# The products of the modulation vectors on VectorE, one multiply-add per piece, instead of two GpSimd operations

## The chip, the cores and the metric

The kernel runs on one core of a Trainium2 chip. The metric is the device time of one execution in microseconds. Three runs of the kernel before took 4000.06, 3992.86 and 4002.28 us; their median is 4000.06 us.

## What is computed

Two model blocks follow each other on one sequence of 512 tokens and 1024 channels, all in float32. The first has a feed-forward part, a mixer (chunked attention beside a gated recurrence) and a second feed-forward part. The second has two layers, each a mixer of four branches (Fourier, differential attention, grouped attention, convolution) and a feed-forward part; beside it runs a context sequence of 256 tokens. Each of the parts is wrapped in a normalisation whose shift, scale and gate are vectors that depend on a conditioning vector alone:

```
c_act = silu(c)
mod = (c_act @ w_ada[l] + b_ada[l]).reshape(b, N_SUB, 3, D_MODEL)
...
def sandwich(x, fn, g_pre, g_post, shift, scale, gate, res_w):
    h = modulate(rmsnorm(x, g_pre), shift, scale)
    y = rmsnorm(fn(h), g_post)
    return x + res_w * gate[:, None, :] * y
...
mod_x = (jax.nn.silu(c) @ w_mod[l] + b_mod[l])[:, None, :]
mod_c = (jax.nn.silu(c_ctx) @ w_mod[l] + b_mod[l])[None, None, :]
```

A modulation vector is thus one row of 1024 numbers: a vector of 1024 times a matrix of 1024x1024. The kernel computes 29 of them. The first two are made in a start routine (L392) that the change leaves alone; the other 27 go through `mod` and `pieces`.

## The kernel before

**Matrix products.** Each float32 weight is split in two: a high part (`whi`, written by ScalarE, L282) and the rest (`wlo`, written by VectorE as raw minus high, L283), and each product is three matmuls (L309 to L311, or L321 to L323). The work is a list of `Step`s; a step owns units of weights of 128x1024. `run` (L226) goes through the steps and calls `pump` (L235), which loads units ahead into five `raw` tiles (`RAWB`, L161; the DMA is issued on SyncE's queue, L243) and splits them up to four ahead (`HB`, L162). A `raw` tile is free again when its last reader is done; for a split unit that is the VectorE subtraction of L283.

**A modulation vector.** The matrix is cut in eight pieces of 128 rows, each loaded as one unit of 128x1024 that is not split (`plain`, L390), into the same five `raw` tiles. Piece i is multiplied by column i of the activated conditioning vector (`csil`, one number per partition) and added to an accumulator `a`, a tile `s` of 128x1024. When the eighth piece is in, `turn` (L348) transposes the accumulator in blocks of 32x32 and adds along the row on VectorE (L352, L353), and `fin` (L355) ends it with one matmul, the bias and the gain (L360, L363) and writes the vector to memory by a DMA of GpSimd's queue (L365). `use` (L469) later loads it back, broadcast over the partitions.

**How a piece is multiplied.** `pieces` (L371) takes the engine as an argument and has a branch for either:

```
if i == 0:
    eng.tensor_scalar(a, v, c, 0.0, ALU.mult, ALU.add)
elif eng is self.DVE:
    eng.scalar_tensor_tensor(a, v, c, a, ALU.mult, ALU.add)
else:
    eng.tensor_scalar(v, v, c, 0.0, ALU.mult, ALU.add)
    eng.tensor_tensor(a, a, v, ALU.add)
```

Before the change `mod` passes GpSimd (`self.POOL`, L366): the first piece is one operation (L383), the other seven are two each (L387 into the `raw` tile, L388 into the accumulator). The `raw` tile is free after L388.

**What sets the order.** The vectors of one part are woven between the steps of the part before it (`weave`, L138, by the costs and the shares in `TUNE`). A scheduler then orders the instructions of each engine when the program is built, so a change of one operation's engine can move others. Beside the pieces GpSimd does a taps part of the convolution (L1539, L1540), small powers for the normalisations (L335, L481), some scalings (L1343, L867) and its DMAs, all in one queue.

**Other lines that the prediction names.** L1149 and L1147 are parts of the rotary embedding on VectorE; L328 is the rest of a split of a matmul's result (`esplit`, reads PSUM); L334, L335 and L1440 are a normalisation's factor (VectorE, then GpSimd, then VectorE) that the matmul of L1445 needs; L906 and L908 are the first part's short convolution; L930 to L945 its recurrence.

Of the kernel before, what the change touches and what calls it, by code (L numbers as in the profile page):

```python
# [159 lines left out]
class K:  # L160
# [177 lines left out]
    def mod(self, key, w, c0, bias, ccol, gain=None, mult=None):  # L338

        E, DVE, PE = self.E, self.DVE, self.PE  # L340

        def begin():
            self.cnt += 1
            r = E[key, "r"] = self.sb.tile([32, 2, 32], F32, tag="row", bufs=3, name=f"row{self.cnt}")
            for j, v in enumerate([bias[c0:c0 + D]] + ([gain] if gain is not None else [])):
                self.POOL.dma_start(out=r[:, j, :], in_=v.rearrange("(a b) -> a b", a=32))

        def turn(raw):  # L348

            a, v = E.pop((key, "a")), raw[:, 0, :]  # L350
            q = E[key, "q"] = self.sb.tile([128, 32], F32, tag="red", bufs=3, name=f"red{self.cnt}")
            DVE.transpose(v, a)  # L352
            DVE.tensor_reduce(q, v.rearrange("p (a b) -> p a b", b=32), AX, ALU.add)  # L353

        def fin():  # L355
            q, r = E.pop((key, "q")), E.pop((key, "r"))
            ps = self.mm((32,))[0:32, :]
            PE.matmul(ps, q, self.fold, start=True, stop=True)
            v = r[:, 0, :]
            DVE.tensor_tensor(v, ps, v, ALU.add)  # L360
            if gain is not None:
                o = (1.0, ALU.add) if mult is None else (mult, ALU.mult)
                DVE.scalar_tensor_tensor(v, v, o[0], r[:, 1, :], o[1], ALU.mult)  # L363
            d = E[key, "d"] = self.dr.tile([32, 32], F32, tag="d" + key, name="d" + key)
            self.POOL.dma_start(out=d, in_=v)  # L365
        steps = self.pieces(key, w, c0, ccol, begin, self.POOL)  # L366
        u = steps[-1].units
        steps[-1].units, steps[-1].borrow = [], u
        return steps + [Step(turn, u, need=(), pe=0.1), Step(fin, pe=0.1)]
# [113 lines left out]
    def border(self, xk, T, yk=None, out=None, norm=None, hk=None):  # L483
# [34 lines left out]
        def tr(t):  # L518
# [14 lines left out]
            for g in range(2):  # L533
                if T == S:
                    self.esplit(ps[g], hT[:, 0, 4 * g:4 * g + 4, ts], hT[:, 1, 4 * g:4 * g + 4, ts])
                else:
                    for q in range(2):
                        self.esplit(ps[g][:, 2 * q:2 * q + 2, :], hT[2 * g + q][:, 0, :, ts], hT[2 * g + q][:, 1, :, ts])
        return first, mod, tr

    def calls(self, *cs, **kw):
# [1414 lines left out]
```

## Time and profile before

| | |
|---|---|
| median of three runs | 4000.06 us (3992.86 to 4002.28) |
| the profiled execution's own time | 4003.47 us |
| its span, first to last instruction | 4001.7 us |
| mean granted TensorE clock | 0.964 of 2.4 GHz |
| TensorE matmuls (PE) busy | 3773.1 us, 94% |
| VectorE (DVE) busy | 2514.3 us, 63% |
| ScalarE (ACT) busy | 1533.9 us, 38% |
| GpSimd (POOL) busy | 1394.0 us, 35% |
| memory traffic | 133 GB/s over the span |

The engines run beside each other; an engine's busy time counts its instructions alone, and its idle time is waiting. A chain of waits says which engine the end hangs on; here it is TensorE nearly throughout. The granted clock is the share of full speed that TensorE was allowed in a stretch; it has two levels, full (2.4 GHz) and half (1.2 GHz), so a mean of 0.9 means that a fifth of the stretch was at half.

### The profile page before, as it was taken

What the parts mean: (1) busy time and instruction counts of PE and PEld (TensorE: products, weight loads), DVE (VectorE), ACT (ScalarE), POOL (GpSimd) and SP (SyncE); (2) the same over time, 40 slices, a digit from 0 to 9 for tenths busy, and PEclk for the clock granted to TensorE, in tenths of its full rate; (3) what the DMA queues carried; (4) which work ended last, traced back from release to release, by engine and by line L of the source; (5) the groups of instructions that cost most, each with busy time, mean ns of one, the idle gap of its engine ahead of it and who ended that gap; (6) DMA issues with size and microseconds to landing.
All of it is one profiled execution on the core that took longest, in us unless ns stands there. A gap on an engine that the chain in (4) does not pass through costs nothing. (4 is left out here: it accounts for less than half of the span.)

```text
span 4001.7 us, 50668 instructions
## 1 busy us (share of the span) xinstructions
PE 3773.1 (94%) x19612; PEld 3196.3 (80%) x19612; DVE 2514.3 (63%) x3347; ACT 1533.9 (38%) x2437; POOL 1394.0 (35%) x1133
## 2 busy tenths in 40 slices
PE   7999987999899999899999989999998999899999
PEld 5888866778788887778887878888887887688887
DVE  5343478846766665957667466767587776655344
ACT  4222345533354443235433334333332543334322
POOL 1341364315844332451323144543146132312100
PEclk9999988999999999999999989999999999899999
DMA  6554533446455655221333356666532123333432
GB/s 226 155 160 128 152 113 116 145 127 194 149 160 173 187 168 176 80 82 41 106 95 95 121 166 198 195 200 195 170 104 82 56 85 96 106 121 114 127 103 94
DMA packets 534050, 536.26 MB, mean 134 GB/s; under 512 B 19696, under 2 KB 435696, under 8 KB 533808
## 3 DMA queue, kind: packets, MB, share of 16 engines
q1 hardware_dynamic: 517088, 487.48, 40.1%
q0 software_dynamic: 16720, 45.53, 3.5%
q8 instruction: 154, 2.52, 0.3%
q14 instruction: 88, 0.72, 0.1%
HBM read 507.66 MB, written 25.28 MB: 133 GB/s over the span
## 5 line engine op out<-in xcount | busy, mean ns | idle before, releaser
L283 DVE TENSOR_TENSOR wlo<-raw,whi 128x1024 fp32r<-128x1024 f32 (+3 forms) x674 | 921.9, 1370 | 803.1 <-ACT whi L282 783.6
L282 ACT ACTIVATE whi<-raw 128x1024 fp32r<-128x1024 f32 (+3 forms) x674 | 694.1, 1032 | 1551.6 <-PE mm L310 649.5
L309 PE MATMUL mm<-hT,whi 128*128 128x512 f32 (+1 forms) x2384 | 910.8, 385 | 44.4 <-ACT hT L326 11.0
L310 PE MATMUL mm<-hT,whi 128*128 128x512 f32 (+1 forms) x2384 | 907.1, 382 | 17.9 <-DVE hT L328 17.9
L311 PE MATMUL mm<-hT,wlo 128*128 128x512 f32 (+1 forms) x2384 | 902.9, 380 | 0.0
L309 PEld LDWEIGHTS mm<-hT,whi 128*128 128x128 f32 x2384 | 460.4, 195 | 132.4 <-ACT hT L326 14.0
L310 PEld LDWEIGHTS mm<-hT,whi 128*128 128x128 f32 x2384 | 463.2, 195 | 99.3 <-DVE hT L328 20.5
L311 PEld LDWEIGHTS mm<-hT,wlo 128*128 128x128 f32 x2384 | 462.6, 194 | 83.4 <-issue 0.4
L388 POOL TENSOR_TENSOR s<-s,raw 128x1024 f32<-128x1024 f32 x189 | 495.6, 2622 | 15.8
L387 POOL TENSOR_SCALAR raw<-raw,csil 128x1024 f32<-128x1024 f32 x189 | 281.4, 1489 | 380.9 <-DMA raw<-in_w_mod 191.2
L322 PE MATMUL mm<-wlo,s 128*128 128x512 f32 (+1 forms) x1004 | 371.4, 371 | 4.6 <-DVE wlo L283 4.6
L321 PE MATMUL mm<-whi,s 128*128 128x512 f32 (+1 forms) x1004 | 369.1, 371 | 0.0
L323 PE MATMUL mm<-whi,s 128*128 128x512 f32 (+1 forms) x1004 | 368.9, 370 | 0.0
L309 PE MATMUL mm<-s,whi 128*128 128x256 f32 (+1 forms) x1032 | 338.1, 329 | 10.9 <-ACT s L910 5.1
L310 PE MATMUL mm<-s,whi 128*128 128x256 f32 (+1 forms) x1032 | 333.1, 323 | 3.0 <-DVE s L328 3.0
L311 PE MATMUL mm<-s,wlo 128*128 128x256 f32 (+1 forms) x1032 | 332.0, 322 | 0.0
L309 PEld LDWEIGHTS mm<-s,whi 128*128 128x128 f32 x1032 | 199.2, 193 | 31.7 <-ACT s L910 5.5
L326 ACT ACTIVATE s<-mm 128x512 fp32r<-128x512 f32 (+2 forms) x302 | 156.7, 548 | 172.6 <-PE mm L1027 67.8
L322 PEld LDWEIGHTS mm<-wlo,s 128*128 128x128 f32 x1004 | 189.8, 189 | 37.1 <-DVE wlo L283 5.5
L321 PEld LDWEIGHTS mm<-whi,s 128*128 128x128 f32 x1004 | 189.8, 189 | 33.2 <-ACT eh L708 0.5
L323 PEld LDWEIGHTS mm<-whi,s 128*128 128x128 f32 x1004 | 189.8, 189 | 32.1 <-DVE s L690 0.4
L310 PEld LDWEIGHTS mm<-s,whi 128*128 128x128 f32 x1032 | 199.7, 194 | 19.2 <-DVE s L328 3.4
(334 smaller groups left out, 6179.6 us busy)
## 6 DMA issues: line engine op xcount, KB each, us to landing
raw<-in_w_in SPq DMA_DIRECT2D x231, 512.0 KB, 4.0
raw<-in_w_ff SPq DMA_DIRECT2D x188, 512.0 KB, 4.3
raw<-in_w_mod SPq DMA_DIRECT2D x160, 512.0 KB, 4.0
raw<-in_ffn_w_gu SPq DMA_DIRECT2D x88, 512.0 KB, 4.2
raw<-in_w_ada SPq DMA_DIRECT2D x72, 512.0 KB, 3.9
raw<-in_ffn_w_down SPq DMA_DIRECT2D x42, 512.0 KB, 3.8
raw<-in_w_out SPq DMA_DIRECT2D x32, 512.0 KB, 3.7
d_x<-s POOLq DMA_DIRECT2D x28, 512.0 KB, 4.8
```

The lines of the kernel that those rows point to most:

```text
L282: self.ACT.activation(hi, v, ACTF.Copy)
L283: self.DVE.tensor_tensor(lo, v, hi.bitcast(F32), ALU.subtract)
L309: self.PE.matmul(out, hi[:, k, j:j + c], ah, start=start and k == 0, stop=False)
L310: self.PE.matmul(out, hi[:, k, j:j + c], al, start=False, stop=False)
L311: self.PE.matmul(out, lo[:, k, j:j + c], ah, start=False, stop=stop and k == nk - 1)
L321: self.PE.matmul(o, ah, hi[:, k, :], start=start and k == 0 and t % per == 0, stop=False)
L322: self.PE.matmul(o, ah, lo[:, k, :], start=False, stop=False)
L323: self.PE.matmul(o, al, hi[:, k, :], start=False, stop=stop and k == nk - 1 and t % per == per - 1)
L326: self.ACT.activation(hi, ps, ACTF.Copy, scale=scale)
L387: eng.tensor_scalar(v, v, c, 0.0, ALU.mult, ALU.add)
L388: eng.tensor_tensor(a, a, v, ALU.add)
```

## The change

`mod` passes VectorE instead of GpSimd to `pieces`, so that the other branch is taken: the first piece is one VectorE operation (L383), each other piece one VectorE multiply-add (L385), `a = v * c + a`. L387 and L388 are no longer issued. Nothing else is edited.

```diff
@@ -363,7 +363,7 @@
                 DVE.scalar_tensor_tensor(v, v, o[0], r[:, 1, :], o[1], ALU.mult)
             d = E[key, "d"] = self.dr.tile([32, 32], F32, tag="d" + key, name="d" + key)
             self.POOL.dma_start(out=d, in_=v)
-        steps = self.pieces(key, w, c0, ccol, begin, self.POOL)
+        steps = self.pieces(key, w, c0, ccol, begin, self.DVE)
         u = steps[-1].units
         steps[-1].units, steps[-1].borrow = [], u
         return steps + [Step(turn, u, need=(), pe=0.1), Step(fin, pe=0.1)]
```

How it moves instructions is read at three places. The numbers behind the tiles' names are the build's own and differ between the two programs.

First, GpSimd's queue around the power of a normalisation in the second layer's mixer (L335; `st` is the factor, `s` the accumulator of a vector). Before:

```order
L387 TENSOR_SCALAR raw_28142<-raw_28142,csil 128x1024
L388 TENSOR_TENSOR s_27958<-s_27958,raw_28142 128x1024
L335 TENSOR_TENSOR st_28454<-st_28454,mhalf 128x4
L387 TENSOR_SCALAR raw_28152<-raw_28152,csil 128x1024
L388 TENSOR_TENSOR s_27958<-s_27958,raw_28152 128x1024
```

And VectorE's queue at the same place now, from L334, which feeds that power, to L1440, which uses it:

```order
L334 TENSOR_SCALAR st_28281<-mm_28276 128x4
L1149 TENSOR_TENSOR s_28245<-s_28245,eh_28256 128x256
L283 TENSOR_TENSOR wlo_28521<-raw_28350,whi_28520 128x1024
L1149 TENSOR_TENSOR s_28245<-s_28245,eh_28261 128x256
L328 TENSOR_TENSOR s_28294<-mm_28289,s_28294 128x512
L328 TENSOR_TENSOR s_28302<-mm_28297,s_28302 128x512
L1440 TENSOR_SCALAR e_28284<-ident,st_28281 128x128 x4
```

GpSimd had pieces ahead of the power and behind it; VectorE has no piece between L334 and L1440. That vector's last pieces stand earlier in VectorE's queue.

Second, VectorE's queue in the first block's recurrence (`s_4618` is a vector's accumulator, `s_4561` and `s_4314` belong to the recurrence). Now:

```order
L283 TENSOR_TENSOR wlo_4605<-raw_4451,whi_4604 128x256
L385 SCALAR_TENSOR_TENSOR s_4618<-raw_4379,csil,s_4618 128x1024
L930 SCALAR_TENSOR_TENSOR s_4561<-s_4561,s_4314 128x512
L1058 TENSOR_TENSOR eh_4548<-mm_4539,eh_4548 64x256
L385 SCALAR_TENSOR_TENSOR s_4618<-raw_4612,csil,s_4618 128x1024
L931 SCALAR_TENSOR_TENSOR s_4561<-s_4561 128x512
L1063 TENSOR_TENSOR s_4440<-eh_4548,s_4440 64x256
L385 SCALAR_TENSOR_TENSOR s_4618<-raw_4616,csil,s_4618 128x1024
L943 SCALAR_TENSOR_TENSOR s_4561<-s_4314,s_4561 128x512
```

Here pieces stand between the operations of a chain; before, none of the three was in VectorE's queue.

Third, the last feed-forward part, where a piece stands right behind a split. SyncE's queue of loads (the same order before and now), and then VectorE's queue now:

```order
L243 DMA raw_30440<-in_w_ff_2 128x2x512
L243 DMA raw_30470<-in_w_ff_2 128x2x512
L243 DMA raw_30500<-in_w_ff_2 128x512
L243 DMA raw_30503<-in_w_ff_2 128x8x128
L243 DMA raw_30529<-in_w_ff_2 128x8x128
L243 DMA raw_30561<-in_w_mod 128x1024
```

```order
L283 TENSOR_TENSOR wlo_30497<-raw_30380,whi_30496 128x1024
L283 TENSOR_TENSOR wlo_30526<-raw_30440,whi_30525 128x1024
L385 SCALAR_TENSOR_TENSOR s_30190<-raw_30561,csil,s_30190 128x1024
L283 TENSOR_TENSOR wlo_30558<-raw_30470,whi_30557 128x1024
```

With five `raw` tiles, the piece `raw_30561` is loaded into the tile that `raw_30440` leaves, and VectorE's very next instruction after the split that frees it is the piece itself.

## Rows read from the trace of the kernel before

**Rows 1.** The page's head: span, and busy time of the engines.
```profile
span 4001.7 us, 50668 instructions
PE 3773.1 (94%) x19612; PEld 3196.3 (80%) x19612; DVE 2514.3 (63%) x3347; ACT 1533.9 (38%) x2437; POOL 1394.0 (35%) x1133
```

**Rows 2.** Stretches: length, busy us (instructions) by engine, granted clock, DMA share, GB/s.
```profile
500.00:760.00 260.00, 219.72 (x934) 173.28 (x933) 220.05 (x311) 142.79 (x246) 140.38 (x118) 0.88 0.40 120
930.00:1120.00 190.00, 172.81 (x987) 151.54 (x986) 142.89 (x194) 70.14 (x117) 148.15 (x121) 0.95 0.55 166
1120.00:1560.00 440.00, 437.55 (x2568) 384.03 (x2568) 281.02 (x383) 200.04 (x325) 150.88 (x107) 1.00 0.60 181
1960.00:2170.00 210.00, 188.44 (x1091) 161.44 (x1091) 146.47 (x223) 73.17 (x126) 84.69 (x51) 0.91 0.37 109
...
2400.00:2790.00 390.00, 386.29 (x2064) 333.23 (x2062) 268.16 (x268) 155.21 (x222) 173.93 (x102) 1.00 0.64 197
3280.00:3500.00 220.00, 195.07 (x1124) 164.88 (x1124) 146.84 (x226) 74.49 (x128) 76.94 (x46) 0.91 0.37 108
```

**Rows 3.** Groups of GpSimd: operation xcount | busy us, mean ns | idle before, releasers.
```profile
L388 POOL TENSOR_TENSOR s<-s,raw 128x1024 f32<-128x1024 f32 x189 | 495.6, 2622 | 15.8
L387 POOL TENSOR_SCALAR raw<-raw,csil 128x1024 f32<-128x1024 f32 x189 | 281.4, 1489 | 380.9 <-DMA raw<-in_w_mod 191.2 <-DMA raw<-in_w_ada 68.7 <-issue 56.3
...
L383 POOL TENSOR_SCALAR s<-raw,csil 128x1024 f32<-128x1024 f32 x27 | 35.8, 1325 | 137.3 <-DMA raw<-in_w_ada 51.2 <-DMA raw<-in_w_mod 37.2 <-PE mm L1052 26.6
```

**Rows 4.** Three VectorE lines: xcount: duration ns min/median/max.
```profile
L283 DVE TENSOR_TENSOR wlo<-raw,whi x674: 398/1225/3440, 37.2 to 3972.5; 128x1024 fp32r<-128x1024 f32 x161, 128x768 fp32r<-128x768 f32 x6, 128x256 fp32r<-128x256 f32 x1, 128x512 fp32r<-128x512 f32 x1
...
L1149 DVE TENSOR_TENSOR s<-s,eh x32: 403/412/2555, 1947.2 to 3426.5; 128x256 f32<-128x256 f32 x32
...
L328 DVE TENSOR_TENSOR s<-mm,s x274: 275/679/694, 478.9 to 3547.9; 128x512 fp32r<-128x512 f32 x110, 128x256 fp32r<-128x256 f32 x21, 128x128 fp32r<-128x128 f32 x6
```

**Rows 5.** Timeline from 3423 us, GpSimd then VectorE: start us, us, what.
```profile
3424.37 1.11 POOL L387 TENSOR_SCALAR raw<-raw,csil 128x1024 f32<-128x1024 f32 x1
3425.56 3.19 POOL L388 TENSOR_TENSOR s<-s,raw 128x1024 f32<-128x1024 f32 x1
...
3430.11 2.34 POOL L388 TENSOR_TENSOR s<-s,raw 128x1024 f32<-128x1024 f32 x1
...
3424.70 1.86 DVE L283 TENSOR_TENSOR wlo<-raw,whi 128x1024 fp32r<-128x1024 f32 x1 [1.24 <-ACT whi L282]
3426.48 2.56 DVE L1149 TENSOR_TENSOR s<-s,eh 128x256 f32<-128x256 f32 x1
...
3430.16 2.37 DVE L1440 TENSOR_SCALAR e<-ident,st 128x128 f32<-128x128 f32 x1
```

**Rows 6.** TensorE's waits from 3280 to 3500 us: us in total, times, longest.
```profile
PE mm L1445 <- DVE e L1440: 10.9, 1, 10.9
```

**Rows 7.** The start routine's VectorE products: xcount: duration ns min/median/max.
```profile
L407 DVE SCALAR_TENSOR_TENSOR s<-raw,csil,s x14: 1275/1285/1352, 7.0 to 32.3; 128x1024 f32<-128x1024 f32 x14
...
L405 DVE TENSOR_SCALAR s<-raw,csil x2: 747/750/753, 5.7 to 16.1; 128x1024 f32<-128x1024 f32 x2
```

**Rows 8.** Waits of SyncE's queue of loads: us in total, times, longest.
```profile
SPq L243 <- DVE wlo L283: 2484.4, 545, 24.8
SPq L243 <- POOL s L388: 325.1, 91, 12.3
```

**Rows 9.** Timeline from 3733 us, VectorE then SyncE's queue: start us, us, what.
```profile
3735.93 1.23 DVE L283 TENSOR_TENSOR wlo<-raw,whi 128x1024 fp32r<-128x1024 f32 x1 [1.98 <-ACT whi L282]
3740.88 1.23 DVE L283 TENSOR_TENSOR wlo<-raw,whi 128x1024 fp32r<-128x1024 f32 x1 [3.73 <-ACT whi L282]
...
3737.18 0.34 SPq L243 DMA_DIRECT2D raw<-in_w_mod  x1
```

**Rows 10.** The page's loads of the pieces: xcount, KB each, us to landing.
```profile
raw<-in_w_mod SPq DMA_DIRECT2D x160, 512.0 KB, 4.0
...
raw<-in_w_ada SPq DMA_DIRECT2D x72, 512.0 KB, 3.9
```

## The prediction

> **What bounds the kernel now.** I read the page's head first, then the stretches, then VectorE's and GpSimd's lines, and last the timeline of one wait. The head shows TensorE's matmuls busy 3773.1 of 4001.7 us and VectorE at 63%, GpSimd at 35% [rows 1]: no engine but TensorE is near full, so time can be won only where TensorE waits, and where its clock is down after a wait. The stretches tell where that is [rows 2]. While feed-forward parts run (1120 to 1560 us, 2400 to 2790 us) TensorE is busy 437.55 of 440 and 386.29 of 390 us at clock 1.00, though GpSimd multiplies pieces there too. In four other stretches, the mixers in which pieces are multiplied (from 500, 930, 1960 and 3280 us), it lacks 40.3 + 17.2 + 21.6 + 24.9 = 104 us of 880, and the granted clock is 0.88, 0.95, 0.91 and 0.91: at half clock work takes twice as long, so the loss is about (1 - clock) x length = 31.2 + 9.5 + 18.9 + 19.8 = 79 us. **104 + 79 = 183 us is what the change can touch at all.**
>
> Why TensorE waits there is seen in the timeline. GpSimd's L387 starts at 3424.37 and lasts 1.11 us; VectorE's split L283, started at 3424.70, takes 1.86 us instead of its median 1.225 [rows 4, 5]. L388 runs from 3425.56 to 3428.75; L1149, median 0.412 us, takes 2.56 and ends 0.29 us after it. The next L388 runs from 3430.11 to 3432.45, and L1440, started in its shadow, takes 2.37. TensorE waits for L1440 through all of this, 10.9 us [rows 6]. The held time is 0.63 + 2.15 + at most 2.3 us, nearly half of that wait. Over the whole run the same shows in the durations: L283 reaches 3.44 us and L1149 2.56, but L328, which reads PSUM, never exceeds 0.694 in 274 instructions [rows 4]. So VectorE operations that read SBUF are held while a GpSimd piece runs, and those that read PSUM are not.
>
> **The change part by part.** GpSimd loses L387, L388 and L383: 281.4 + 495.6 + 35.8 = 813 us of busy time [rows 3], and falls from 1394 to about 581 us. It isn't the bound, so this alone is worth nothing. What follows from it is:
>
> (a) The holds by the pieces end. In the four stretches I give them half of what TensorE loses, as in the wait above: half of 183, 92 us (52 of waits, 40 of clock). The bounds: nothing, if every wait is as long with its other causes alone (some end on ScalarE or on TensorE's own results); three quarters, 137 us, if a held operation also delays what stands behind it in a full queue, as VectorE has it from 500 to 760 us (220 of 260 us busy) [rows 2].
>
> A different reading of the slow operations would be that the two engines share a path at half speed each; then an operation of 0.41 us could at most double, and the term would be under half of this. The 2.56 us of L1149 speak against it [rows 5]. The Trainium skill, "SBUF — State Buffer", section "Who interferes with whom", says that a VectorE instruction with two SBUF inputs, or in a mode that uses two ports, and a GpSimd instruction that reads SBUF contend for one port pair, and that the later one is blocked until the first is through. By that rule the term is the 92 us, by sharing it would be some 40; the trace agrees with the lock.
>
> (b) VectorE gains 27 first pieces and 189 multiply-adds. The start routine has both operations at this size: 0.750 and 1.285 us [rows 7]. That is 27 x 0.750 + 189 x 1.285 = 263 us, 2514 + 263 = 2777 us or 69% of the span at most; every hold that ends comes off this. In the four stretches 12 of the 27 vectors are multiplied, 12 x (0.75 + 7 x 1.285) = 117 us. The bounds of what this costs TensorE are 0 (all of it in VectorE's idle time) and 117 us or more (all of it ahead of something awaited). Between them I go by the rows: VectorE works 220 + 143 + 146 + 147 = 656 us in these stretches and TensorE waits 104, so a microsecond of VectorE work has so far come to at most 0.16 us of waiting, and with the clock (183 / 104) to 0.28. 117 x 0.28 = **33 us given back**. The order bears out that this is nearer the low end: between L334 and L1440, the wait above, no piece is left, while in the recurrence three stand inside the chain. The other 15 vectors fall where TensorE is 97% busy or more; the cover there is the up to four units split ahead. In 2400 to 2790 us it is some 103 splits, one in 3.8 us, so about 15 us of lead; the cover gone, they would cost 15 x 9.75 = 146 us.
>
> (c) Loads start earlier. SyncE's queue waited 325 us for L388 to free a tile, 91 times [rows 8]; a `raw` tile is now free after one VectorE operation. L352 no longer waits for GpSimd. TensorE's own waits there name neither a load nor L352: 0.
>
> (d) A wait is added: in VectorE's queue each piece now waits for its own load, and what is queued behind it (splits, softmax, normalisations) waits with it. GpSimd stood idle 380.9 us before L387, mostly for loads [rows 3]. The third place of the order shows it at its worst: the load of a piece is issued at 3737.18, as the split of 3735.93 ends, and lands 3.9 to 4.0 us later [rows 9, 10]; VectorE has nothing in between. The next split started at 3740.88, so it loses only the piece's own time. Over the order, by the trace's durations of what lies between, 80 of 216 pieces stand less than 4.0 us of VectorE work behind the instruction that frees their tile, 168 us in all, but only 13 us of that in the four stretches; the other 155 lie where TensorE has its lead. 0, with the bound in the second rival.
>
> **Sum.** -92 + 33 = -59 us against the profiled execution's own 4003.47 us gives 3944.5; that execution was 3.4 us above the median of the runs, so in their terms 3941. I say **3942 us**, 1.5% less.
>
> **The rivals.**
>
> 1. *The work only changes places.* VectorE does for itself what it was held for: 117 us of pieces in the four stretches against holds of the same size, and the waits stay. 4000 us. For it: the sums are alike. Against it: holds strike whatever happens to run, pieces stand where the scheduler put them. 0.13.
>
> 2. *VectorE waits for loads, and TensorE for VectorE.* The place is the feed-forward parts, where pieces stand right behind the split that frees their tile. If half of those 155 us reached TensorE, 78 us would come on top of -59: 4020 us. It decides from 59 / 155 = 38% on. For it: VectorE is one queue, and a late split delays the next load too. Against it: TensorE's lead of some 15 us over waits of at most 4. 0.15.
>
> 3. *VectorE becomes the bound in the first mixer.* It has 40 us idle from 500 to 760 us [rows 2] and gets 4 x 9.75 = 39 us. If no hold ended there, it would be full, and the stretch would grow by the 39 us: 4039 us. It needs the holds to be no part of the 220 us, against [rows 4]. 0.05. The Trainium skill, "Perfetto Trace Analysis", section "Optimizing Scalar/DVE Operations", says that moving work from a saturated VectorE to ScalarE or even GpSimd may pay, though the shared port may undo it; by its first half this rival holds. No row shows VectorE saturated without pieces beside it.
>
> 4. *More than half of the waits were holds.* Three quarters of 183 us go and little comes back: 3865 us. For it: with VectorE 85% busy from 500 to 760 us a hold there has little slack to vanish in. Against it: the wait above was held for less than half. 0.10.
>
> **How the numbers follow.** My forecast has 0.57, and its own range, by the bounds of (a) and (b), is 3890 to 3988. About 0.3% (12 us) is what a measurement can tell from no change here. Faster: 0.57 + 0.10 = 0.67; the same: 0.13; slower: 0.15 + 0.05 = 0.20. The range of eight in ten goes from 3865, the fourth rival's time, to 4010, which leaves out most of the second and third and some of the fourth's low side.
>
> **What would show it.** Right: L387 and L388 gone, GpSimd near 580 us; L283's mean near its median of 1.225 us, and L1149's maximum far below 2.5; L385 189 times at 1.285 us; VectorE's busy time within 60 us of 2514; TensorE waiting some 25 us less in the four stretches together with fewer half-clock slices; the 10.9 us wait for L1440 about halved. Wrong: a new group of VectorE idle time ended by the loads of `in_w_mod` and `in_w_ada`, with TensorE below 97% in 1120 to 1560 or 2400 to 2790 us (second rival); the four stretches unchanged with L283 at its median (first); the stretch from 500 us longer, with VectorE over 95% (third).

## The result, and the profile after

The changed kernel takes **3925.88 us** (median of four runs, 3922.41 to 3931.64) against 3999.66 us: a ratio of 0.982 with an interval of 0.9802 to 0.9837, 74 us less. The prediction was 3942.

The head of the page, as [rows 1]:

```profile
span 3924.9 us, 50381 instructions
...
PE 3744.3 (95%) x19612; PEld 3182.0 (81%) x19612; DVE 2481.3 (63%) x3563; ACT 1533.9 (39%) x2437; POOL 596.1 (15%) x728
```

GpSimd lost 798 us and VectorE, with 216 operations more, works 33 us less, though its new work is 264 us (below). So held VectorE time is gone: 2514 + 264 - 2481 = 297 us by busy time. Busy time counts the overlap of two successive operations once, and the 264 us do not; by added durations, which the trace gives too, it is 2681.6 + 264 - 2672.7 = **273 us**.

The stretches, cut at the same TensorE instructions as [rows 2] (columns as there; the fifth, 2313.90, answers to 2360 to 2400 us before, which was not among the rows):

```profile
500.80:734.60 233.80, 210.62 (x934) 169.65 (x933) 197.44 (x344) 142.20 (x246) 28.67 (x58) 0.91 0.46 137
904.00:1082.00 178.00, 166.72 (x987) 147.63 (x986) 136.89 (x213) 69.28 (x116) 87.53 (x90) 0.97 0.60 179
1082.00:1521.60 439.60, 436.42 (x2569) 382.93 (x2568) 273.18 (x411) 200.86 (x326) 31.51 (x48) 1.00 0.60 180
1921.30:2122.90 201.60, 188.40 (x1092) 160.72 (x1091) 152.16 (x248) 72.98 (x125) 6.35 (x10) 0.93 0.39 117
2313.90:2337.60 23.70, 23.70 (x114) 19.89 (x113) 18.62 (x25) 10.43 (x18) 0.00 (x0) 1.00 0.73 225
2337.60:2726.20 388.60, 386.49 (x2064) 333.73 (x2064) 253.87 (x308) 155.41 (x226) 17.45 (x30) 1.00 0.64 198
3213.30:3423.60 210.30, 192.02 (x1124) 163.61 (x1123) 157.80 (x252) 74.05 (x128) 7.32 (x10) 0.92 0.39 118
```

The four stretches of the prediction are 26.2 + 12.0 + 8.4 + 9.7 = 56 us shorter. TensorE lacks 66 us in them and not 104, and (1 - clock) x length is 57 us and not 79. The feed-forward stretches are as they were. The fifth row is the surprise: the same matmuls took 40.0 us before and take 23.7 now, with TensorE never idle.

VectorE's durations (xcount: ns min/median/max), as [rows 4, 7], and the idle time ahead of the pieces:

```profile
L283 DVE TENSOR_TENSOR wlo<-raw,whi x674: 410/1224/2310, 38.0 to 3895.8; 128x1024 fp32r<-128x1024 f32 x161, 128x768 fp32r<-128x768 f32 x6, 128x256 fp32r<-128x256 f32 x1, 128x512 fp32r<-128x512 f32 x1
L1149 DVE TENSOR_TENSOR s<-s,eh x32: 402/416/426, 1908.4 to 3351.9; 128x256 f32<-128x256 f32 x32
L385 DVE SCALAR_TENSOR_TENSOR s<-raw,csil,s x189: 1257/1284/1784, 111.0 to 3737.1; 128x1024 f32<-128x1024 f32 x189
L383 DVE TENSOR_SCALAR s<-raw,csil x27: 741/748/974, 108.6 to 3608.6; 128x1024 f32<-128x1024 f32 x27
```
```profile
L385 DVE SCALAR_TENSOR_TENSOR s<-raw,csil,s 128x1024 f32<-128x1024 f32 x189 | 243.5, 1288 | 173.6 <-DMA raw<-in_w_mod 112.4
```

The new work is 243.5 + 27 x 0.748 = 264 us. L1149's maximum fell from 2.555 to 0.426. The new wait of VectorE for loads is there, 174 us ahead of L385. SyncE's queue, as [rows 8]; L388's 325 us are gone, and the pieces' new readers take part of their place:

```profile
SPq L243 <- DVE wlo L283: 2424.7, 553, 24.9
SPq L243 <- DVE s L385: 186.2, 131, 4.3
...
SPq L243 <- DVE s L383: 95.1, 26, 21.3
```

The wait for L1440 [rows 5, 6], now (GpSimd, VectorE, TensorE):

```profile
3350.59 1.15 POOL L335 TENSOR_TENSOR st<-st,mhalf 128x4 f32<-128x4 f32 x1 [26.46 <-DVE st L334]
...
3350.75 1.22 DVE L283 TENSOR_TENSOR wlo<-raw,whi 128x1024 fp32r<-128x1024 f32 x1
3351.89 0.42 DVE L1149 TENSOR_TENSOR s<-s,eh 128x256 f32<-128x256 f32 x1
3352.22 1.28 DVE L328 TENSOR_TENSOR s<-mm,s 128x512 fp32r<-128x512 f32 x2
3353.42 0.86 DVE L1440 TENSOR_SCALAR e<-ident,st 128x128 f32<-128x128 f32 x4
...
3354.43 2.05 PE L1445 MATMUL mm<-e,ones 128*128 128x512 f32 x2 [3.86 <-DVE e L1440]
```

The same VectorE operations, none held; 3.86 us instead of 10.92.

**The place that the prediction did not have.** The kernel before, 2360 to 2400 us: first the window (columns as above), then TensorE's waits there and SyncE's from 2330 to 2372 us (total, times, longest), then the timeline of ScalarE, SyncE's queue, VectorE and GpSimd:

```profile
2360.00:2400.00 40.00, 30.60 (x115) 22.96 (x114) 20.89 (x20) 10.58 (x19) 23.54 (x15) 0.83 0.60 175
```
```profile
PE big L321 <- ACT whi L282: 3.8, 2, 3.4
PE mm L532 <- ACT s L574: 3.3, 1, 3.3
...
SPq L243 <- DVE wlo L283: 45.1, 7, 24.7
```
```profile
2377.43 1.06 ACT L282 ACTIVATE whi<-raw 128x1024 fp32r<-128x1024 f32 x1 [5.63 <-DMA raw<-in_w_ff]
2386.90 1.06 ACT L282 ACTIVATE whi<-raw 128x1024 fp32r<-128x1024 f32 x1 [8.42 <-DMA raw<-in_w_ff]
...
2352.60 14.01 SPq L243 DMA_DIRECT2D raw<-in_w_ff  x2
2366.67 5.42 SPq L243 DMA_DIRECT2D raw<-in_w_mod  x2
2372.18 0.39 SPq L243 DMA_DIRECT2D raw<-in_w_ff  x1
...
2356.84 4.03 DVE L509 TENSOR_TENSOR s<-s,s 128x768 f32<-128x768 f32 x2
2360.79 4.34 DVE L516 SCALAR_TENSOR_TENSOR s<-s,st,s 128x512 f32<-128x512 f32 x2
2365.05 1.21 DVE L283 TENSOR_TENSOR wlo<-raw,whi 128x1024 fp32r<-128x1024 f32 x1
2366.19 4.34 DVE L516 SCALAR_TENSOR_TENSOR s<-s,st,s 128x512 f32<-128x512 f32 x2
...
2371.05 0.68 DVE L283 TENSOR_TENSOR wlo<-raw,whi 128x512 fp32r<-128x512 f32 x1
...
2359.14 2.63 POOL L387 TENSOR_SCALAR raw<-raw,csil 128x1024 f32<-128x1024 f32 x1
2361.86 2.72 POOL L388 TENSOR_TENSOR s<-s,raw 128x1024 f32<-128x1024 f32 x1
```

TensorE waits for ScalarE: for a split, and for L574, which stands right behind the split of 2386.90 in ScalarE's queue; both splits had waited for loads of weights. Going back from there: of the two loads in SyncE's first row the second went out only at 2366.29, as VectorE's split of 2365.05 ended and freed a tile, and that split stood behind two pairs of held operations (4.03 and 4.34 us; in the changed kernel the same pairs take 1.82 and 1.41), with GpSimd's pieces running beside them. The load that the split of 2377.43 waited for stands further back in SyncE's queue. It went out at 2372.18, behind a piece's load that had waited for VectorE's split of 2371.05, and that split stood behind a third pair, 4.34 us. So a hold reaches TensorE here through two queues and some 10 to 20 us later. TensorE lacks 40 - 30.6 = 9.4 us and, at clock 0.83, 6.8 more: 16.2 us, which is what this place gained.

### The profile page after: what moved, and what is told of

The parts are those of the page before. It is cut to its first block, busy times and chain, and to the rows that moved or that the text cites. A ratio compares the mean times of both kernels' runs of the same rounds, so it can differ in the third digit from the quotient of the medians.

```text
span 3924.9 us, 50381 instructions
## 1 busy us (share of the span) xinstructions
PE 3744.3 (95%) x19612; PEld 3182.0 (81%) x19612; DVE 2481.3 (63%) x3563; ACT 1533.9 (39%) x2437; POOL 596.1 (15%) x728
## 5 line engine op out<-in xcount | busy, mean ns | idle before, releaser
L283 DVE TENSOR_TENSOR wlo<-raw,whi 128x1024 fp32r<-128x1024 f32 (+3 forms) x674 | 816.5, 1214 | 676.7 <-ACT whi L282 666.4
L385 DVE SCALAR_TENSOR_TENSOR s<-raw,csil,s 128x1024 f32<-128x1024 f32 x189 | 243.5, 1288 | 173.6 <-DMA raw<-in_w_mod 112.4
L326 ACT ACTIVATE s<-mm 128x512 fp32r<-128x512 f32 (+2 forms) x302 | 157.4, 548 | 151.2 <-PE mm L1027 66.4
L310 PEld LDWEIGHTS mm<-s,whi 128*128 128x128 f32 x1032 | 199.3, 193 | 15.8 <-issue 1.0
L311 PEld LDWEIGHTS mm<-s,wlo 128*128 128x128 f32 x1032 | 198.9, 193 | 14.2
```

Of the source, the lines that this page charges most:

```text
L283: self.DVE.tensor_tensor(lo, v, hi.bitcast(F32), ALU.subtract)
L310: self.PE.matmul(out, hi[:, k, j:j + c], al, start=False, stop=False)
L311: self.PE.matmul(out, lo[:, k, j:j + c], ah, start=False, stop=stop and k == nk - 1)
L326: self.ACT.activation(hi, ps, ACTF.Copy, scale=scale)
```

## The experiments

The question was what the 74 us are made of. Theory: long GpSimd operations hold VectorE (term a), less what VectorE's new work costs (term b). Rivals: tiles that come free sooner (term c, put at 0), and work that only changes places. The kernel before, run beside each, had 3999.1 to 3999.8 us. Every build is ordered anew by the scheduler: of the 3347 VectorE operations that the kernel before has too, some 340 stand elsewhere in the order of the changed kernel, and some 60 to 230 in the runs made from the kernel before. What the order alone is worth was not run.

**Neither holds nor added work.** In the kernel before:

```diff
-eng.tensor_scalar(v, v, c, 0.0, ALU.mult, ALU.add)
-eng.tensor_tensor(a, a, v, ALU.add)
+eng.tensor_scalar(v[:, :16], v[:, :16], c, 0.0, ALU.mult, ALU.add)
+eng.tensor_tensor(a[:, :16], a[:, :16], v[:, :16], ALU.add)
```

> Kernel before, with GpSimd's two operations of the pieces after the first cut to 16 of 1024 columns; the rest of those products is left out. Neither the holds nor the added VectorE work are in it, and a raw tile comes free as soon as its load has landed. Holds theory (term a, with b = 33 us given back): -74 measured = a + 33, so a is -107 and this kernel runs in 3893 us. Rival 1, the added VectorE work costs nothing: the same as the changed kernel, 3926. Rival 2, the added work costs its full 117 us in the four stretches: 3809 or less. VectorE's busy time should be about 2481 - 263 = 2218 us.

3902.18 us (0.9757, 0.9742 to 0.9771). Both rivals fall, and the holds theory is 9 us off. The pieces on GpSimd cost 97 us in all; on VectorE they cost 3926 - 3902 = **24 us**. VectorE works 2254.7 us here (2218 expected), so 227 us of its time cost 24, or 0.10 each. The 27 first pieces are still on GpSimd in this run, so the 24 us are what VectorE's new work costs less what those 27 cost.

**Holds kept, tiles free sooner.** Behind the two short operations, two long ones on the accumulator:

```diff
+eng.tensor_scalar(a, a, self.ones[:, 0:1], 0.0, ALU.mult, ALU.add)
+eng.tensor_tensor(a, a, a, ALU.add)
```

> Like the run with 16 columns, but behind each pair GpSimd does two operations of the full 128x1024 on the accumulator alone (times one, and plus itself); the products' other columns are again left out. GpSimd is as busy as in the kernel before (1394 us and the short operations more), so the holds stay, but a raw tile is free about 4 us sooner than there. Holds theory: within 12 us of the kernel before, 3988 to 4010 us. Rival, the gain came from tiles that come free sooner (term c, which was put at 0): a good part of the 74 us is seen here, 3930 to 3960. If only the place before 2400 us hung on the late loads: 3984.

3947.05 us (0.9869, 0.9854 to 0.9885), 52 less than before, which the expectation would put down to the tiles. But the long add took less than L388 does, so the holds were not kept whole. The next run adds another tile in its place (`a8` is `a` in eight parts, `i8` the identity repeated):

```diff
-eng.tensor_tensor(a, a, a, ALU.add)
+eng.tensor_tensor(a8, a8, i8, ALU.add)
```

> Like the run with two long operations on the accumulator, but the second adds the identity's tile, repeated, instead of the accumulator itself, so that it reads two different tiles and should take the 2.4 us of L388 and not 1.9. The products' columns past 16 are again left out. Holds as long as in the kernel before, raw tiles free as soon as two short operations are done. Holds theory: what is left of the gain is what early tiles bring, 97 - 75 = 22 us: 3970 to 3985. Rival, early tiles brought the 52 us of the run before and the length of the operation does not matter: 3947 again. If the second operation is no longer than 1.9 us this run tells nothing new.

3976.61 us (0.9941, 0.9927 to 0.9955): 22.5 us less than before. The add in the kernel before, in the first of these two runs and in the second (ns min/median/max):

```profile
L388 POOL TENSOR_TENSOR s<-s,raw x189: 2340/2409/3431, 82.8 to 3815.2; 128x1024 f32<-128x1024 f32 x189
```
```profile
L390 POOL TENSOR_TENSOR s<-s x189: 1891/1895/2972, 82.4 to 3760.0; 128x1024 f32<-128x1024 f32 x189
```
```profile
L391 POOL TENSOR_TENSOR s<-s,ident x189: 2338/2408/3462, 84.0 to 3792.3; 128x1024 f32<-128x1024 f32 x189
```

With holds of full length, earlier tiles bring 22 us; half a microsecond less of each long add brought 30 more. These 30 us are the cleanest sign of the holds: VectorE, ScalarE and SyncE have their instructions in the same order in the two runs, and VectorE's busy time is 2484.5 us with the longer add and 2411.6 with the shorter. Of the 97 us at most 75 are holds, since GpSimd's queue is still as long as before and what it costs is in these 75 too.

**Tiles late, no long holds.** One short multiply and eleven short adds on the raw tile, one behind the other:

```diff
+for _ in range(11):
+    eng.tensor_tensor(a[:, :16], a[:, :16], v[:, :16], ALU.add)
```

> Kernel before, with each of the 189 pieces after a vector's first done by GpSimd in twelve short operations on 16 columns, one behind the other (about 0.3 us each, 3.5 us together, about as long as L387 and L388 are unheld); the products' other columns are left out. The raw tile comes free as late as before and GpSimd's queue is as long, but no operation is long enough to hold VectorE for more than some 0.3 us. The run with two short operations was 97 us under the kernel before, the one with long operations on the accumulator 52. If long holds are most of it (some 75 of the 97): 3915 to 3935 us. Rival, tiles that come free late and GpSimd's own queue are most of it: 3970 to 3990. VectorE's L283 mean near 1.23 in the first case and in the second.

3937.26 us (0.9842, 0.9829 to 0.9856): 62 us less than before, just past the expected range, with VectorE 2256.5 us busy, 258 less. The other 35 of the 97 are the time that a piece spends on GpSimd. From the start of its first operation to the end of its last that is 4.73 us on average here, 4.19 in the kernel before and 0.90 in the run with two short operations, so 35 is if anything high and 62 low. SyncE's waits only changed their releaser:

```profile
SPq L243 <- DVE wlo L283: 2316.6, 502, 24.9
SPq L243 <- POOL s L389: 295.2, 95, 15.9
SPq L243 <- POOL raw L387: 183.5, 53, 9.7
```

For GpSimd it is 479 us against 325, for L283 2317 against 2484 [rows 8].

**Tile or queue.** Ten of the eleven short adds moved from the raw tile to the accumulator alone:

```diff
+    eng.tensor_tensor(a[:, :16], a[:, :16], a[:, 16:32], ALU.add)
```

> Like the run with twelve short operations per piece, but only the first two touch the raw tile; the other ten work on the accumulator alone, on 16 columns. GpSimd's queue is as long as there (about 3.5 us per piece), the raw tile comes free early. The products' other columns are left out. The run of twelve on the tile stood at 3937, the run of two at 3902: 35 us that are either late tiles or GpSimd's own queue (powers and scalings that wait behind a piece). If late tiles: 3902 to 3910. Rival, the queue: 3930 to 3940. The run with full holds and early tiles, 22 us under the kernel before, says that tiles are at least 22 of the 35: 3902 to 3915.

3922.82 us (0.9806, 0.9793 to 0.9819), between the two and in none of the expected ranges. 14 of the 35 us go with the tile of the piece itself, 21 with the queue. Since the next piece waits in that queue with its own tile, the 21 are late tiles as well as other GpSimd work that waits, and which of the two stays open.

This run gives the holds a second time. It and the run with full holds both free the tile early and keep GpSimd's queue (4.77 and 5.26 us a piece on average); they differ by 3976.61 - 3922.82 = 54 us, with VectorE 230 us less busy. So two pairs of runs give 54 and 62 us, and 75 is the most: **54 to 75 us are holds, 22 to 43 the pieces' time on GpSimd.**

**More work on VectorE.** In the changed kernel:

```diff
-eng.scalar_tensor_tensor(a, v, c, a, ALU.mult, ALU.add)
+eng.tensor_scalar(v, v, c, 0.0, ALU.mult, ALU.add)
+eng.tensor_tensor(a, a, v, ALU.add)
```

> Changed kernel, with each of the 189 multiply-adds done by VectorE in two operations (multiply into the raw tile, add). VectorE gets 189 x (0.75 + 1.225 - 1.285) = 130 us more, 58 of it in the four stretches. By the prediction's 0.28: 16 us slower than the changed kernel, 3942. Rival 1, VectorE's added work costs nothing: 3926. Rival 2, each added microsecond there is paid: 3984. If the wait of VectorE for loads matters, longer pieces do not lengthen it.

3961.05 us (0.9903, 0.9886 to 0.9919): 35 us slower than the changed kernel for 112 us of VectorE time (2592.9 - 2481.3), 0.31 each and twice what was expected. The price of VectorE's time is not one slope: the first 227 us cost 0.10 each, the next 112 three times as much. In this run a piece also keeps its `raw` tile for two operations instead of one, and what that costs is in the 0.31.

**The remaining long GpSimd work.** In the changed kernel the third channel of the convolution as the other two:

```diff
-elif c < 2:
+elif c < 3:
     DVE.scalar_tensor_tensor(acc, vp[:, j:j + T], wc, acc, ALU.mult, ALU.add)
```

> Changed kernel, and the third channel's 90 taps of the convolution, too, are one VectorE multiply-add each instead of two GpSimd operations. GpSimd loses 220 us more (596 to about 376), VectorE gains 60 x 0.742 + 30 x 0.47 = 59 us and loses what the other channels' taps were held for (mean of the 512-column form 0.935 against a median of 0.74). Holds theory: the waits for L1540 (8.3 us) go and those for L1163 shrink, 10 to 20 us faster than the changed kernel: 3905 to 3916. Rival, the taps' stretches have VectorE on the path and the work only changes places: 3920 to 3940.

**3886.70 us** (0.9717, 0.9702 to 0.9731), 39 us faster than the changed kernel, twice what was expected, and the best kernel of this study. The head's row, and the taps before this edit and after it:

```profile
PE 3725.8 (96%) x19612; PEld 3169.0 (82%) x19612; DVE 2470.9 (64%) x3653; ACT 1534.0 (39%) x2437; POOL 375.9 (10%) x548
```
```profile
L1536 DVE SCALAR_TENSOR_TENSOR s<-s,dwh,s x180: 464/741/1782, 963.8 to 2962.1; 128x512 f32<-128x512 f32 x120, 128x256 f32<-128x256 f32 x60
```
```profile
L1536 DVE SCALAR_TENSOR_TENSOR s<-s,dwh,s x270: 442/737/752, 966.3 to 2961.6; 128x512 f32<-128x512 f32 x90, 128x256 f32<-128x256 f32 x45
```

VectorE has 90 operations more and works 10 us less.

**Going on with it** did not pay. On top of that kernel: (1) L509's 256 columns and L589 to VectorE too, (2) the first mixer's vectors begun later:

```diff
-XS = 256
+XS = 0
...
-(POOL if ch == 0 else DVE).tensor_tensor(y, o, gain, ALU.mult)
+DVE.tensor_tensor(y, o, gain, ALU.mult)
```
```diff
-"mods": [(0.12, 0.96, 1.0), (0, 0.88, 1.0),
+"mods": [(0.12, 0.96, 1.0), (0.2, 0.94, 1.0),
```

> The run with all taps on VectorE, and two more of GpSimd's operations there: the 256 columns of L509 (30 times, 1.4 us each) and L589 (18 times, 1.34 us each). GpSimd loses 66 us, VectorE gains 30 x 0.33 + 18 x 0.69 = 22 us. VectorE's operations are held by hardly more than 10 us in all there, so both theories say the same within 12 us: 3880 to 3895 us; holds theory 3882, work that only changes places 3890.

> The run with all taps on VectorE, with the vectors that are woven into the first mixer begun a fifth of the part later (0.2 to 0.94 of it instead of 0 to 0.88). From 500 to 600 us the pieces on VectorE cost 15 us (changed kernel against the run without them), from 600 to 760 us nothing: if they cost there because VectorE has the softmax to do, beginning later gives some 10 of the 15 us back: 3875 to 3880 us. Rival, they cost wherever they stand in this mixer: 3885 to 3892.

3910.06 us (0.9775, 0.9762 to 0.9788) and 3893.12 (0.9735, 0.9722 to 0.9749): 23 and 6 us slower. The first was expected by neither theory. VectorE's busy time grew by 13 us alone, so more than the work was lost; its trace loses 3 to 4 us in each of the four stretches, and why was not tried. In the second, the matmuls of 500 to 600 us took 7 us less and those of 600 to 760 us took 7 more: the pieces cost wherever they stand in this mixer.

**A sixth raw tile** needs the room of a buffer `e` (`RAWB = 6`, `ne=5`), on the best kernel and on the kernel before:

> The run with all taps on VectorE, with five instead of six of the buffers e (2 KB of a partition each): the room that a sixth raw tile needs. It is there as the base of that run. If a buffer of the softmax is short without it: 3900 to 3930; otherwise 3887.

> The run with all taps on VectorE, with five buffers e and a sixth raw tile. If tiles are still short with the pieces on VectorE (it waits some 170 us for the loads of pieces), the sixth takes most of these waits away and gives up to 10 us against the run with five buffers e alone. Rival: these waits lie where TensorE has its lead, so nothing (within 6 us).

> Kernel before, pieces on GpSimd as they were, with five buffers e and a sixth raw tile. If tiles that come free late are 22 to 35 us of what the pieces on GpSimd cost, a sixth tile brings back a good part: 10 to 30 us less than the kernel before, apart from what the buffer costs (the run with five buffers e tells it): 3970 to 3990. Rival, the holds are all and tiles nothing: 3995 to 4005 plus the cost of the buffer.

Without the buffer 3926.64 us (0.982, 0.9806 to 0.9833), 40 slower; with the sixth tile 3915.41 (0.9791, 0.9777 to 0.9805), so the tile gives 11 us, tiles are still short with the pieces on VectorE, and it does not pay for its room. On the kernel before 4011.57 (1.003, 1.0018 to 1.0041). What the buffer alone costs there was not run, so this last run settles nothing on tiles.

**By place.** How much shorter each stretch of the kernel before became, worked out from the start of the TensorE instruction with the same number in the two traces (us; the third row begins 100 us before the prediction's stretch, and up to 1960 us only "two ops" differs, by 1 us; "none" is the run with two short operations, "late tiles" that with twelve on the tile, "queue" that with ten of the adds moved off the tile, "holds" that with full holds and earlier tiles, "two ops" VectorE's two operations, "taps" the best kernel):

| us before | changed | none | late tiles | queue | holds | two ops | taps |
|---|---|---|---|---|---|---|---|
| 500 to 760 | 26.1 | 42.2 | 37.4 | 36.2 | 6.1 | 12.6 | 23.8 |
| 930 to 1120 | 12.0 | 7.8 | 4.6 | 4.9 | -3.8 | 8.2 | 15.8 |
| 1860 to 2170 | 8.5 | 15.7 | 13.0 | 15.4 | 11.4 | 1.2 | 9.1 |
| 3280 to 3500 | 9.9 | 12.4 | 10.2 | 12.6 | 9.9 | 7.8 | 13.0 |
| 2360 to 2400 | 16.2 | 16.2 | 9.3 | 15.0 | 1.6 | 16.2 | 16.2 |
| 1120 to 1560 | 0.5 | -0.7 | -5.9 | -4.2 | 1.7 | -3.9 | -0.5 |
| 2400 to 2790 | 1.6 | 4.2 | -3.1 | 2.0 | -0.5 | 1.4 | 3.0 |
| 1650 to 1860 | -0.1 | 0.0 | 1.3 | -0.3 | -0.2 | -4.1 | 21.5 |
| whole span | 76.7 | 100.4 | 65.2 | 76.8 | 24.8 | 37.5 | 117.1 |

## Why the prediction was right, and where it was not

The direction and the mechanism held, and the sum was short by 16 us. That it came so near is partly luck. In the four stretches it said 92 - 33 = 59 us and 56 came, but 56 is 45 to 65 us of holds, 13 to 33 of the pieces' time on GpSimd, less 22 for VectorE's work: a term too large, one left out and one too costly cancel.

- **(a), the holds: 92 us forecast in the four stretches, 45 to 65 measured there** (54 to 75 in the whole kernel). By the table, "late tiles" gains 65 us in these stretches without long holds, and "queue" 45 more than "holds". The step that failed is "I give them half of what TensorE loses, as in the wait above". That one wait fell by 7.1 of its 10.9 us, more than half; others kept their other cause: in the first mixer the longest wait, 8.9 us for ScalarE's L326 before, is 8.2 now. That a held operation is locked out and not slowed to half speed is borne out by durations: 2.56 us of L1149 before against 0.426 at most now, and the 9.07 us in the last section. The 30 us of the shorter adds fit both readings.
- **(b), VectorE's work: 33 forecast, 24 measured** (22 in the four stretches: 78.1 without pieces, 56.5 with). The 0.28 was too high for this amount of work and near the price of the next 112 us.
- **The four stretches were not all.** The step that failed is "104 + 79 = 183 us is what the change can touch at all": 2360 to 2400 us, with its 16.2 us, was left out, and all of it went. It is as much as the forecast lacked. Without long holds that place gains 9.3 us with late tiles and 15.0 with early ones ("queue"), with full holds 1.6.
- **(c), earlier tiles: 0 forecast, 22 to 43 measured** for all that hangs on a piece's time on GpSimd. The step that failed is "TensorE's own waits there name neither a load nor L352: 0": it looked at the four stretches alone and at the last releaser alone, where a late load shows as a late split.
- **(d), VectorE's wait for loads: 168 us forecast, 174 found, and it costs nothing that shows in the feed-forward stretches, where it was feared.** TensorE is busy 99% of both feed-forward stretches, and without pieces on VectorE they are 1.2 us longer and 2.6 us shorter.
- **The sum by measured terms**: -62 - 35 + 24 = -73 us, or with the other splits -54 - 43 + 24 and -75 - 22 + 24; measured -74. This sum has to come out, since its terms are differences between the same runs; it checks nothing.
- **The forecast's own range**, 3890 to 3988, does not follow from the bounds of (a) and (b): these give 4000 - 137 = 3863 to 4000 + 117 = 4117 us.
- **Rivals.** The first (work changes places) falls: 258 us of held time (of the 189 pieces) cost 54 to 75, 264 us of work 24. The second falls with (d). The third too: VectorE is 197 of 234 us busy in the first mixer, 84%, and its step from a full VectorE to 39 us more was never worked out; yet its seed is there, since in the part from 500 to 600 us, worked out like the table, the changed kernel loses 4 us where the run without them gains 12. The fourth is not what happened: less than half of the 183 us were holds.
- **What was to be seen**: GpSimd 596 us (580 forecast), VectorE within 60 us of 2514 (33 less), L283's mean 1.214 us, 38 us less waiting in the four stretches (25).

## What to carry to other kernels

A microsecond of VectorE held by GpSimd cost 0.23 to 0.29 us of time here (54 us for 230, at most 75 for 258), one of VectorE's own work 0.10, so long elementwise work on two SBUF tiles belonged on VectorE even though GpSimd stood mostly idle; the price of VectorE's time then rises (0.31), so go step by step and stop. When costing a queue that frees buffers sooner, follow TensorE's releaser back to the load before writing 0, and look at every short stretch with a clock below 1.00, not only at the long ones.

## What the runs showed of the hardware

The hold goes the other way too, and further. In the run with twelve short operations one add of 16 columns, median 0.221 us, took 9.07 us, from 995.55 to 1004.63. The group of eleven adds in which it stands on GpSimd, and VectorE meanwhile:

```profile
L389 POOL TENSOR_TENSOR s<-s,raw x2079: 216/221/9071, 82.3 to 3753.6; 128x16 f32<-128x16 f32 x189
```
```profile
994.82 12.21 POOL L389 TENSOR_TENSOR s<-s,raw 128x16 f32<-128x16 f32 x11
...
997.45 2.84 DVE L1537 SCALAR_TENSOR_TENSOR s<-s,dwh,s 128x256 f32<-128x256 f32 x7
1000.22 1.21 DVE L283 TENSOR_TENSOR wlo<-raw,whi 128x1024 fp32r<-128x1024 f32 x1
1001.36 1.26 DVE L1537 SCALAR_TENSOR_TENSOR s<-s,dwh,s 128x256 f32<-128x256 f32 x3
1002.54 1.21 DVE L283 TENSOR_TENSOR wlo<-raw,whi 128x1024 fp32r<-128x1024 f32 x1
1003.68 0.86 DVE L1537 SCALAR_TENSOR_TENSOR s<-s,dwh,s 128x256 f32<-128x256 f32 x2
```

VectorE runs operations with two SBUF inputs without a gap until 1004.54, and the add ends 0.09 us later: by these times it was passed over by the whole row of them. In the run with ten adds moved off the tile the longest add, 9.74 us, does the same: it ends at 1006.14, 0.09 us after the last L1538 of such a row (L1537 above), while VectorE is already at an L328, which reads PSUM. The Trainium skill, "SBUF — State Buffer", section "Who interferes with whom", says that the engine that issues second is blocked until the first is done. L1440's hold of one GpSimd operation's length [rows 5] agrees, and this case shows that a held GpSimd operation can wait for many VectorE operations.

A GpSimd add of a tile to itself took 1.895 us, and of two different tiles 2.408, at the same size and type.
